# One attention and FFN layer, its instruction queues ordered by the framework's finer timeline model instead of its default model

## The chip, the cores and the metric

The kernel runs on one core of a Trainium2 chip. Five engines work from queues of their own, each in the order in which its instructions were written into it: TensorE (PE in the profile, with its weight loads as PEld), VectorE (DVE), ScalarE (ACT), GpSimd (POOL) and SyncE (SP), which issues the DMAs. An instruction that needs another engine's result waits on a semaphore, and everything behind it in its queue waits too. The metric is the device time of one execution in microseconds.

## The reference

One layer of a streaming encoder over 1024 positions of width 1024, all in float32. Two kinds of attention run on the same input, eight heads of 64 each:

```python
h = x @ w_in[l]
qa, ka, va, qb, kb, vb, ga, gb = jnp.split(h, split_pts, axis=-1)
y_a = chunk_band_attention(heads_a(qa), heads_a(ka), heads_a(va), rel_bias[l]) @ w_proj_a[l]
y_b = stick_breaking_attention(heads_b(qb), heads_b(kb), heads_b(vb)) @ w_proj_b[l]
gate_a = jax.nn.sigmoid(ga + b_gate[l, :D])
gate_b = jax.nn.sigmoid(gb + b_gate[l, D:])
mix = (gate_a * y_a + gate_b * y_b) @ w_out[l]
x = layer_norm(DEEPNORM_ALPHA * x + mix, ln1_g[l], ln1_b[l])
g, u = jnp.split(x @ w_ffn_in[l], 2, axis=-1)
x = layer_norm(DEEPNORM_ALPHA * x + (jax.nn.silu(g) * u) @ w_ffn_out[l], ln2_g[l], ln2_b[l])
```

Branch A is a softmax over a band of nine chunks of 64 keys with a learned bias by distance. Branch B is stick-breaking attention: the weight of a key is its sigmoid times the product of (1 - sigmoid) over the keys between it and the query, so it needs a running product along the keys.

## The kernel before, in words

Positions are stored backwards, so that a running product goes from left to right. For precision, each float32 operand of a product is split into a high part and a low remainder (`split`, L109 on ACT for the high part, L110 on DVE for the remainder), and a product is three matmuls: high by high, high by low, low by high. A matmul here has 128 x 128 weights and up to 512 columns.

The work goes in these stages, one after the other in the program's text:

1. *Input projection* (L171, tiles sxp, syp, szp). Blocks of columns of `w_in` are taken in pairs and multiplied by a scheme with seven products in place of eight (`pair_steps`). Pair 0 is multiplied plainly (L116 to L119, tile plain). The results q, k and v go to DRAM (q_dr, k_dr, v_dr), the first ten gate blocks too (g_dr).
2. *Attention*, sixteen heads: a0 to a7, then b0 to b7. Each head has eight *weight units* of 128 queries and twelve *value steps* of 128 keys.
   - A unit of branch A (`soft_block`): scores on TensorE (L464, L465, tile sc_a, PSUM banks of the tag sc, of which there are two), a DVE instruction that adds the bias and takes the row's minimum (L495), the exponential on ACT (L500), a reciprocal on DVE (L502), a scaling on POOL (L503).
   - A unit of branch B (`stick_block`): scores (tile sc_b), two sigmoids on ACT (L528, L529), the running products on DVE (L532, L536), a product on POOL (L538).
   - A value step: up to four transposes of weight blocks on TensorE (L561, tile tp), the split into pt (L109 on ACT, L110 on DVE), then two matmuls with v (L574, L575, tile pv). The two matmuls are written two steps behind their transposes (`LAG`). At a head's end ACT copies the sums out (L589), and a DMA and POOL join the halves into y (L590, L593, y_dr).
   - *Filler*: matmuls that belong to no head and are dealt out between the value steps by `fill_until`. There are 480: six gate blocks (L421, tile gps, 288 matmuls, each block with a weight load, a split by L404 and L405 and an eviction by L424), and the output product of branch A (L621, tile yAps, 192 matmuls), which needs the finished y of all eight heads of branch A, read back by `reload_y` (L644 to L648). `FILL = (18.0, 42.0)` gives 18 matmuls of filler to each head of branch A and 42 to each of branch B.
3. *Output product of branch B* and the gated sum (tile yBps, then L753, L754), *output projection* (tile ops), the first LayerNorm (POOL L769, ACT L777, POOL L778), and transposes of its result (L791, tile x1ps).
4. *Up projection* (tiles sxf, syf, szf), again with seven products for eight, 21 pairs and one plain block.
5. *Down projection* (L1049, tiles dx, dy, dz, with eighteen blocks by the seven-product scheme and four plain ones, tile fps), the second LayerNorm, and the output.

What sets the order: the program's text gives each instruction its place, and the framework's scheduler then orders each engine's queue. It lets the program run in a model that has a duration for each instruction, and at each point it takes, for an engine that is free, the earliest instruction of the text whose operands and tile slots are ready in the model. So the text's order is a priority and the model's durations decide who is ready. Tile slots are shared through tags (`SLOTS`, `BANKS`), and a later tile waits until the earlier one in its slot has been read for the last time.

## Time and profile before

| what | value |
|---|---|
| time of three runs | 1463.01, 1465.48, 1467.61 us, median 1465.48 |
| span of the profiled execution | 1464.5 us |
| TensorE busy | 1429.5 us (98%), 6740 matmuls |
| DVE busy | 1035.9 us (71%) |
| ACT busy | 679.2 us (46%) |
| POOL busy | 278.8 us (19%) |
| mean share of the 16 DMA engines | 50.6% for the one queue of the kernel's DMAs |
| mean granted TensorE clock | 0.997 |

The page gives no time for the profiled execution beside its span; the span is 1.0 us under the median of the runs. Matmuls are pipelined, so the duration of one overlaps its neighbours, and busy time of TensorE can be near 100% in a stretch where its matmuls start later than they could. The work of stretches is therefore better read from start times.

How the rows are read: in a group, "x96" is the number of instructions, then busy us and the mean ns of one, then idle time of the engine just before them and who ended it. In a row of a stretch, its length in us comes first, then busy us and the number of instructions of PE, PEld, DVE, ACT and POOL, then the granted clock, the DMA share and GB/s. In a row of the timeline or of the chain, the start and the length in us come first.

### The profile page before, as it was taken

How to read it: one execution, taken by the hardware profiler on the slowest of the kernel's cores; microseconds unless marked ns; L12 is line 12 of the kernel's file. 1: busy time of each engine (PE TensorE's matmuls, PEld its weight loads, DVE VectorE, ACT ScalarE, POOL GpSimd, SP SyncE). 2: the span in 40 equal slices, each digit the busy share in tenths (PEclk: the TensorE clock that was granted, in tenths of full speed). 3: DMA queues.
4: the chain of work that ended last, by engine and by line, in shares of the span. 5: the costliest groups of instructions: out<-in, count | busy, mean ns of one | idle time of the engine just before them, and what ended most of it. 6: DMA issues, size and time to landing. Idle time of an engine off the chain costs nothing.

```text
span 1464.5 us, 19170 instructions
## 1 busy us (share of the span) xinstructions
PE 1429.5 (98%) x6740; PEld 1181.3 (81%) x6740; DVE 1035.9 (71%) x1693; ACT 679.2 (46%) x1179; POOL 278.8 (19%) x326
## 2 busy tenths in 40 slices
PE   8999999999999998999999999999999999999997
PEld 6788888887888787777888888888888888888886
DVE  8856655434776987887848966777776665978767
ACT  6444444334887878775413534444444433221201
POOL 0000000003555779760004100000000000100016
PEclk9999999999999999999999999999999999999999
DMA  6555545328666476747611123444444456886602
GB/s 216 158 188 173 160 142 177 125 100 246 194 191 203 123 224 186 236 170 254 235 43 72 50 95 130 158 154 148 152 151 145 155 190 248 304 306 237 212 15 101
DMA packets 83455, 247.72 MB, mean 169 GB/s; under 512 B 10512, under 2 KB 10512, under 8 KB 83360
## 3 DMA queue, kind: packets, MB, share of 16 engines
q1 hardware_dynamic: 83360, 246.51, 50.6%
q8 instruction: 53, 0.87, 0.2%
q14 instruction: 42, 0.34, 0.1%
HBM read 162.03 MB, written 80.77 MB: 166 GB/s over the span
## 4 chain that ended last, share of the span: by engine, by line
PE 83%; DVE 7%; DMA 4%; ACT 2%; issue 2%; POOL 1%; SPq 0%; POOLq 0%; DVEq 0%; ACTq 0%
PE sxf L171 15%; PE sxp L171 12%; PE szf L171 8%; PE szp L171 6%; PE dx L1049 6%; PE syf L171 4%; PE gps L421 3%; PE dz L1049 3%; PE syp L171 3%; PE ops L119 2%; PE ops L117 2%; PE ops L116 2%; PE yAps L621 2%; PE dy L1049 1%; PE tp_b L561 1%
## 5 line engine op out<-in xcount | busy, mean ns | idle before, releaser
L1005 POOL TENSOR_TENSOR wdyt<-wdyt 128x512 f32<-128x512 f32 x8 | 10.9, 1366 | 513.6 <-DVE wdgt L1004 473.4
L538 POOL TENSOR_TENSOR w_b<-w_b,kp_b 128x511 f32<-128x511 f32 (+3 forms) x96 | 96.8, 1018 | 33.6 <-DVE kp_b L536 28.5
L536 DVE TENSOR_TENSOR_SCAN kp_b<-kp_b,ident_ps 128x384 f32<-128x384 f32 (+6 forms) x88 | 78.4, 891 | 7.0 <-ACT kp_b L528 2.2
L482 POOL MEMSET bias<- 64x64 f32 x8 | 1.2, 144 | 329.2 <-ACT bias L481 329.2
L184 DVE TENSOR_TENSOR c<-sxp,c 128x512 f32<-128x512 f32 x16 | 11.1, 692 | 74.6 <-issue 41.4
L769 POOL TENSOR_TENSOR mv<-mv,neghalf 128x1 f32<-128x1 f32 x16 | 23.8, 1489 | 209.4 <-DVE mv L768 209.4
L528 ACT ACTIVATE kp_b<-sc_b 128x512 f32<-128x512 f32 (+3 forms) x96 | 50.3, 525 | 24.0 <-PE sc_b L465 21.7
L110 DVE TENSOR_TENSOR pt_b<-tp_b,pt_b 128x512 fp32r<-128x512 f32 (+1 forms) x96 | 50.1, 541 | 12.5 <-ACT pt_b L109 12.3
L980 DVE TENSOR_TENSOR x<-dx,x 128x512 f32<-128x512 f32 x64 | 43.5, 687 | 17.0 <-PE dx L1049 16.9
L171 PE MATMUL szf<-x1S63h,wcf 128*128 128x512 f32 x168 | 55.1, 389 | 0.0
L109 ACT CAST pt_b<-tp_b 128x512 fp32r<-128x512 f32 (+1 forms) x96 | 48.4, 517 | 7.9 <-PE tp_b L561 7.3
L110 DVE TENSOR_TENSOR sl<-h,sl 128x512 fp32r<-128x512 f32 x56 | 38.4, 686 | 18.9 <-ACT sl L109 18.9
L503 POOL TENSOR_SCALAR w_a<-w_a,st_a 128x640 f32<-128x640 f32 (+2 forms) x64 | 42.6, 667 | 48.0 <-DVE st_a L502 29.7
L561 PE MATMUL tp_b<-ident,w_b 128*128 128x128 f32 x288 | 47.9, 275 | 3.4 <-DVE pt_b L110 3.1
L110 DVE TENSOR_TENSOR pt_a<-tp_a,pt_a 128x512 fp32r<-128x512 f32 (+1 forms) x96 | 46.0, 487 | 7.1 <-ACT pt_a L109 5.9
L529 ACT ACTIVATE w_b<-sc_b 128x511 f32<-128x511 f32 (+3 forms) x96 | 50.6, 527 | 0.0
L109 ACT CAST sl<-h 128x512 fp32r<-128x512 f32 x56 | 34.7, 619 | 33.5 <-PE syf L171 17.1
L116 PE MATMUL ops<-wh_o,mh 128*128 128x512 f32 x128 | 50.2, 392 | 0.0
L119 PE MATMUL ops<-wh_o,ml 128*128 128x512 f32 x128 | 50.0, 391 | 0.0
L117 PE MATMUL ops<-wl_o,mh 128*128 128x512 f32 x128 | 49.9, 390 | 0.0
L109 ACT CAST pt_a<-tp_a 128x512 fp32r<-128x512 f32 (+1 forms) x96 | 39.9, 425 | 19.2 <-PE tp_a L561 18.3
L500 ACT ACTIVATE w_a<-w_a,st_a 128x640 f32<-128x640 f32 (+2 forms) x64 | 44.7, 698 | 7.4 <-DVE st_a L495 5.7
(1883 smaller groups left out, 4796.5 us busy)
## 6 DMA issues: line engine op xcount, KB each, us to landing
s_dr<-sl SPq DMA_DIRECT2D x112, 256.0 KB, 2.2
sd<-s_dr SPq DMA_DIRECT2D x56, 512.0 KB, 4.8
wLf<-in_w_ffn_in_dram SPq DMA_DIRECT2D x22, 512.0 KB, 4.5
wRf<-in_w_ffn_in_dram SPq DMA_DIRECT2D x22, 512.0 KB, 3.5
wLp<-in_w_in_dram SPq DMA_DIRECT2D x17, 512.0 KB, 5.3
wRp<-in_w_in_dram SPq DMA_DIRECT2D x17, 512.0 KB, 4.2
v_dr<-v SPq DMA_DIRECT2D x16, 512.0 KB, 4.2
qs<-q_dr SPq DMA_DIRECT2D x16, 512.0 KB, 5.0
```

The lines of the kernel that those rows point to most:

```text
L109: nc.scalar.copy(dst_h, src)
L110: nc.vector.tensor_tensor(dst_l, src, dst_h.bitcast(F32), ALU.subtract)
L116: mm(acc, lh, rh, start=(i == 0), stop=False)
L117: mm(acc, lh, rl, start=False, stop=False)
L119: mm(acc, ll, rh, start=False, stop=(i == n))
L171: mm(acc, lw[:, ks], rx, start=(first and kt == i == 0), stop=(kt == 3 and i == 2), skip_group_check=not first)
L528: nc.scalar.activation(kp[:, c0:e], sc[:, 0:n], AF.Sigmoid, scale=-1.0)
L529: nc.scalar.activation(be[:, m0:e], sc[:, m0 - c0:n], AF.Sigmoid)
L536: nc.vector.tensor_tensor_scan(kp[:, s0:e], kp[:, s0:e], ident_ps()[:, 0:e - s0], kp[:, s0 - 1:s0], ALU.mult, ALU.bypass)
L538: nc.gpsimd.tensor_tensor(be[:, m0:e], be[:, m0:e], kp[:, m0 - 1:e - 1], ALU.mult)
L561: tr(tp[:, (qb - lo_q) * P:(qb - lo_q + 1) * P], wt[qb - q0][:, (kb - qb) * P:(kb - qb + 1) * P], ident)
L1049: mm(acc, a, b, start=(first and i == n == 0), stop=(i == n - 1 == 1), skip_group_check=not first)
```

## The change

One argument of the context that orders the program. The operations, their tiles, their engines and all sizes are the same; the scheduler's model of time is another, so the instructions of each engine's queue, and the semaphore waits that follow from that, stand in another order.

```diff
     o = nc.dram_tensor("out_0_dram", (1, S, D), F32, kind="ExternalOutput").ap()
-    with tile.TileContext(nc) as tc:
+    with tile.TileContext(nc, schedule_with_timeline_sim=True) as tc:
         hybrid_trunk_kernel(tc, **ap, out=o[0])
```

## The prediction

> **What bounds the kernel now.** I read the page first, for the engines' shares and the chain that ended last, then the busy time by stretch of time, then the groups of instructions by line inside the one stretch where TensorE is not full.
>
> ```profile
> span 1464.5 us, 19170 instructions
> PE 1429.5 (98%) x6740; PEld 1181.3 (81%) x6740; DVE 1035.9 (71%) x1693; ACT 679.2 (46%) x1179; POOL 278.8 (19%) x326
> ...
> PE 83%; DVE 7%; DMA 4%; ACT 2%; issue 2%; POOL 1%; SPq 0%; POOLq 0%; DVEq 0%; ACTq 0%
> ```
>
> ```profile
> 145.44 2.72 PE sxp L171 x12
> ```
>
> TensorE is busy 98% of the span and carries 83% of the chain. In the chain by time (second fence: start, length), twelve matmuls of 512 columns take 2.72 us: 0.227 us each is what a 512-column matmul costs when nothing is late. I call that its pitch. The 389 ns that the groups give for one overlaps its neighbours. Pitches of the narrower shapes come from a dense piece of the timeline, as differences of start times:
>
> ```profile
> 510.25 0.28 PE L574 MATMUL pv_b<-pt_b,v 128*128 128x256 f32 x1
> 510.37 0.28 PE L575 MATMUL pv_b<-pt_b,v 128*128 128x256 f32 x1
> ...
> 511.02 0.28 PE L465 MATMUL sc_b<-kl,qs 128*128 128x128 f32 x1
> 511.13 0.62 PE L561 MATMUL tp_b<-ident,w_b 128*128 128x128 f32 x4
> 511.51 0.47 PE L421 MATMUL gps<-xl,wh_g 128*128 128x512 f32 x1
> ```
>
> That is 0.12 us for 256 columns, about 0.09 for 128 and 0.095 for a transpose (four in 0.38); 320 and 384 columns lie between, 0.147 and 0.175. I add these up over any run of matmuls and call the sum the pure TensorE work of it. Now the stretches, one row each (length, then busy time of PE, PEld, DVE, ACT, POOL):
>
> ```profile
> 335.50:439.80 104.30, 100.61 (x591) 85.71 (x590) 73.32 (x266) 76.23 (x189) 53.23 (x73) 1.00 0.70 207
> 439.80:676.00 236.20, 222.91 (x1244) 185.45 (x1242) 188.56 (x362) 185.44 (x409) 163.19 (x208) 0.99 0.62 190
> 676.00:721.10 45.10, 44.89 (x196) 36.10 (x196) 38.30 (x54) 22.23 (x30) 0.00 (x0) 1.00 0.75 267
> 480.00:500.00 20.00, 17.20 (x100) 13.71 (x101) 18.83 (x34) 17.57 (x43) 16.49 (x26) 1.00 0.42 142
> ...
> 590.00:660.00 70.00, 64.59 (x362) 53.92 (x360) 60.03 (x102) 53.31 (x118) 48.10 (x64) 1.00 0.63 197
> 900.00:1200.00 300.00, 300.00 (x1325) 248.10 (x1324) 212.01 (x291) 129.17 (x195) 0.00 (x0) 1.00 0.44 157
> ```
>
> From 900 to 1200 (the up projection) TensorE is full for all 300 us: nothing can be won, only lost. The first three rows are the attention, cut at the 1450th, 2040th, 3280th and 3474th matmul in issue order; I call them stretch 1, 2 and 3. Their pure work is 91.6, 206.3 and 44.0 us, so they lose 12.7, 29.9 and 1.1 us. That is 43.7 us out of about 50 in the whole kernel; by the same sum the first 200 matmuls lose some 7.5, the stretch about the first LayerNorm about 2.5, all else nothing. What the change is worth is decided here.
>
> **What the change moves.** It removes and adds no computation, only the order in each queue differs: 5,396 of 6,740 matmuls stand at another place. Comparing the two instruction orders by kind:
>
> | matmuls | stretch 1 before | stretch 1 after | stretch 2 before | stretch 2 after |
> |---|---|---|---|---|
> | gps (gates, filler) | 96 | 288 | 192 | 0 |
> | yAps (filler) | 0 | 3 | 192 | 189 |
> | scores, branch A | 152 | 88 | 40 | 104 |
> | transposes tp_a | 164 | 90 | 76 | 150 |
> | values pv_a | 124 | 67 | 68 | 125 |
> | all of branch B | 0 | 0 | 672 | 654 |
>
> Before, the filler is dealt out evenly: the middle one of the 288 gps stands at place 2236, the last at 2725. After, they run in one rush from place 1482 to 2028, beside heads a0 to a2. Filler is work that can always run; it covers TensorE while an attention head waits for DVE, ACT and POOL. The other filler can't take its place at once: a yAps needs the y of all four branch A pairs, so places 2029 to 2538 (a3's rest, a4 to a7, half of b0) hold only 18 of them.
>
> *Stretch 1.* Pure work rises from 91.6 to 110.5 us. For each matmul that waits I counted, in both orders, how many matmuls lie between it and the last one that its producers had to wait for. Between places 1500 and 2000 the smallest such distance was 4 before and is 20 after (some 4 us of matmuls), so TensorE should run nearly full. Bounds: 110.5, and 110.5 plus the 12.7 lost there now; six gate weights have to arrive through SP, ACT and POOL in 110 us, against loads of half that. I take 112, nearest to the full rows: **+7.7**.
>
> *Stretch 2.* Pure TensorE work falls from 206.3 to 189.3, but the work of 2.5 branch A heads arrives (64/24 by scores, 74/30 by transposes, 57/24 by values). What eight of them cost the other engines:
>
> ```profile
> L110 DVE TENSOR_TENSOR pt_a<-tp_a,pt_a 128x512 fp32r<-128x512 f32 (+1 forms) x96 | 46.0, 487 | 7.1 <-ACT pt_a L109 5.9
> L495 DVE CUSTOM_DVE_ANT_0 w_a<-sc_a,bias 128x320 f32<-128x320 f32 (+2 forms) x64 | 30.8, 488 | 9.1 <-PE sc_a L465 7.3 <-PE tp_a L561 1.4
> L495 DVE CUSTOM_DVE_ANT_0 w_a<-sc_a,bias,st_a 128x320 f32<-128x320 f32 x32 | 17.6, 549 | 3.1 <-PE sc_a L465 1.8
> L502 DVE RECIPROCAL st_a<-st_a 128x1 f32<-128x1 f32 x64 | 10.4, 162 | 11.5 <-ACT w_a L500 10.8
> L495 DVE DVE_READ_ACCUMULATOR2_ANT st_a<- 128x1 f32 x96 | 8.0, 83 | 0.0
> ...
> L500 ACT ACTIVATE w_a<-w_a,st_a 128x640 f32<-128x640 f32 (+2 forms) x64 | 44.7, 698 | 7.4 <-DVE st_a L495 5.7 <-DVE st_a L502 0.5
> L109 ACT CAST pt_a<-tp_a 128x512 fp32r<-128x512 f32 (+1 forms) x96 | 39.9, 425 | 19.2 <-PE tp_a L561 18.3
> L500 ACT ACTIVATION_READ_ACCUMULATOR w_a<-w_a,st_a 128x1 f32 x64 | 12.1, 190 | 0.0
> L424 ACT COPY gate<-gps 128x512 f32<-128x512 f32 x12 | 7.5, 622 | 0.6 <-PE gps L421 0.6
> L404 ACT CAST wh_g<-wr_g 128x1024 fp32r<-128x1024 f32 x6 | 6.3, 1049 | 5.4 <-DMA wr_g<-in_w_in_dram 5.4
> L589 ACT COPY yv_a<-pv_a 128x512 f32<-128x512 f32 x8 | 4.7, 586 | 0.0
> L589 ACT COPY yt<-pv_a 128x512 f32<-128x512 f32 x8 | 4.6, 580 | 0.0
> ...
> L503 POOL TENSOR_SCALAR w_a<-w_a,st_a 128x640 f32<-128x640 f32 (+2 forms) x64 | 42.6, 667 | 48.0 <-DVE st_a L502 29.7 <-PE sc_a L465 9.4 <-PE tp_a L561 7.8
> L593 POOL TENSOR_TENSOR yt<-yt,yv_a 64x512 f32<-64x512 f32 x16 | 20.6, 1288 | 8.0 <-DMA yv_a<-yt 5.1 <-DMA yt<-yv_a 2.3
> L405 POOL TENSOR_TENSOR wl_g<-wr_g,wh_g 128x1024 fp32r<-128x1024 f32 x5 | 12.0, 2403 | 16.2 <-ACT wh_g L404 16.0 <-PE gps L421 0.2
> ```
>
> DVE: (46.0 + 30.8 + 17.6 + 10.4 + 8.0) / 8 = 14.1 us a head. ACT: 106 / 8 = 13.3. POOL: 63.2 / 8 = 7.9. In return the splits and evictions of four gates leave: ACT 4 × (1.05 + 2 × 0.62) = 9.2, POOL 4 × 2.4 = 9.6. So stretch 2 has to hold, beside 189 on TensorE:
> - DVE 188.6 + 2.5 × 14.1 = 223.9, less about 2 for the end of b7, which now stands behind the cut: 222;
> - ACT 185.4 + 33.2 − 9.2 = 209 (two more table loads, seven instead of five in all, add at most 2.6 and ACT isn't the longest);
> - POOL 163.2 + 19.8 − 9.6 = 173.
>
> The longest load passes from TensorE to DVE. Where TensorE sets the pace, DVE is busy 80% of stretch 2 and 86% of 590 to 660; where DVE sets it, at the start of branch B (480 to 500), 94%, for 20 us. And DVE has no filler: between places 2000 and 3250, 197 waiting matmuls now stand fewer than 12 matmuls behind what they need, against 45 before. I take 90%, the middle of 86 and 94: 222 / 0.90 = 246.7, **+10.5**. Ends: 94% gives 236 (0), 80% gives 278 (+41).
>
> *Stretch 3.* The last value products of b7 come behind the filler's end, and 18 yBps that could cover the drain now stand ahead of it: eviction (0.58), split of yh7 (1.12) and the add between are bare, about 3 us, on 42.2 of pure work: 45, **0**. Bounds −2 and +3.
>
> *Elsewhere.* In the projections, the up projection and the down projection matmuls are reordered within two neighbouring weight pairs, at most 13 us. The smallest distance rises there, from 4 to 7 or more in the input projection, from 12 to 22 in the up projection (12 are 2.7 us, several times the ACT copy or DVE add that they cover), from 18 to 23 in the down projection, so the cover stays: 0. One wait at the head of the up projection falls to 3, up to +1. In the first 60 us the halves of pair 0 are interleaved and three waits on freshly split weights are as bare as before; 0, bounds −4 and +4. Of the DMAs, the gates' loads and stores stand up to 154 us earlier on SP, ahead of the q, k and v loads of a1 to a5, whose slots come 15 to 35 us later, as the heads themselves do; the y reloads and gA loads now stand among the k loads of b0 to b4, and a late one holds up the head behind it. I put that into the 90%.
>
> Sum: 7.7 + 10.5 + 0 = +18.2 us on the profiled 1464.5. The runs' median, 1465.48, is 1.0 above that span; on it the forecast is 1484.
>
> **Rivals.**
> 1. *The order fits, and it gets faster.* The finer model knows the durations better, stretch 1 no longer loses 12.7 us, and in stretch 2 all four engines interleave without waits. Break-even is 385.6 − 112 − 45 = 228.6 us for stretch 2, a DVE share of 97%. Between 480 and 500 DVE 94%, ACT 88% and POOL 82% were busy together, which speaks for it; that it lasted 20 us speaks against. Faster needs less DVE work as well, by early work in stretch 1 that I can't see: at 215 to 224 us the kernel takes 1452 to 1461.
> 2. *No change.* A DVE share of 96 to 99%, 1461 to 1470. That the option does nothing is excluded by the table.
> 3. *TensorE's clock falls in the gaps.* The trace shows that once:
>
> ```profile
> 578.40 0.50 PE L574 MATMUL pv_b<-pt_b,v 128*128 128x512 f32 x1 [3.08 <-ACT yv_b L589]
> ...
> 580.00:582.00 2.00, 2.00 (x8) 1.71 (x7) 1.09 (x3) 2.00 (x5) 2.00 (x2) 0.50 0.06 14
> 582.00:584.00 2.00, 2.00 (x13) 1.82 (x12) 1.39 (x3) 1.61 (x4) 2.00 (x3) 0.84 0.00 0
> ```
>
> After a gap of 3.08 us the granted clock is 0.50 for about 3.4 us: 1.7 us of matmul time lost. TensorE will idle some 57 us in stretch 2 (246.7 − 189.3). In pieces under 3 us that costs nothing; if a third of it falls into six longer gaps, 6 × 1.7 = 10 us, and the kernel takes 1490 to 1515. Against it: only one gap of that length today.
> [...]
>
> **How the numbers follow.** About 0.3% (4.4 us) is what a measurement can tell from no change. The forecast, filler spent early and DVE setting the pace (5 to 41 us slower): 0.64. Rival 3: 0.08. Rival 1: 0.17. Rival 2: 0.11. So slower 0.72, same 0.11, faster 0.17. Range 1458 to 1511: it cuts off the faster end of rival 1 and the slowest of rival 3 and of the 80% end, about 1 in 10 on each side.
>
> **What would show it.** Right: gps rows end near 450 us, TensorE almost without gaps up to there; behind it PE busy near 77% and DVE near 90% until branch B ends; waits of PE on DVE and ACT (pt_a, pt_b, st_a) that hardly exist now. Wrong: stretch 2 under 229 us, or TensorE gaps in the up or down projection, where I put nothing, or a late gate weight in stretch 1.

## The result, and the profile after

The changed kernel takes 1518.18 us (median of 5 runs, 1514.50 to 1524.22) against 1465.68 us of the kernel before in the same comparison: 1.035 times as long, 95% interval 1.0334 to 1.0365. The forecast was 1484 us with a range to 1511. The direction was right, and the size was about a third of the real one: on the profiled spans the change costs 1515.4 - 1464.5 = 50.9 us, and the prediction's sum was 18.2.

First the page of the changed kernel (span, shares of the engines, shares of the chain), then its busy time by stretch, cut at the same matmuls as in the prediction (length, then busy time of PE, PEld, DVE, ACT, POOL, then granted clock, DMA share, GB/s):

```profile
span 1515.4 us, 19144 instructions
PE 1450.7 (96%) x6740; PEld 1191.7 (79%) x6740; DVE 1020.6 (67%) x1693; ACT 679.0 (45%) x1181; POOL 276.3 (18%) x326
...
PE 85%; DVE 6%; DMA 4%; ACT 3%; issue 1%; SPq 1%; POOL 0%; POOLq 0%; DVEq 0%; ACTq 0%
```

```profile
338.10:454.20 116.10, 114.07 (x592) 96.04 (x592) 43.28 (x148) 57.72 (x122) 40.29 (x45) 1.00 0.56 176
454.20:717.50 263.30, 226.28 (x1240) 180.75 (x1239) 210.44 (x473) 202.77 (x474) 174.07 (x235) 0.97 0.59 178
717.50:769.70 52.20, 47.32 (x198) 37.02 (x197) 38.56 (x57) 22.59 (x31) 0.00 (x0) 0.93 0.69 242
```

The page hardly tells the two kernels apart. The stretches do: ahead of the attention 338.1 - 335.5 = +2.6, stretch 1 +11.8, stretch 2 +27.1, stretch 3 +7.1, behind it +2.3; the sum is the 50.9. In stretch 2 DVE is busy 210.4 / 263.3 = 80%, the share that it had before (188.6 / 236.2), so DVE does not set the pace there. The granted clock is below 1.00 now in stretches 2 and 3 (0.97 and 0.93).

What TensorE waits for, in the changed kernel (total us, times, longest):

```profile
PE tp_b L561 <- DVE pt_b L110: 14.0, 27, 1.2
...
PE yAps L621 <- ACT yh L647: 4.7, 2, 3.2
PE tp_a L561 <- DVE pt_a L110: 3.7, 8, 1.4
...
PE yBps L116 <- ACT yh L109: 2.5, 1, 2.5
```

The first of these rows in the kernel before:

```profile
PE tp_b L561 <- DVE pt_b L110: 3.1, 5, 0.9
```

And what ACT waits for from DMAs in the attention, in the changed kernel and then in the kernel before:

```profile
ACT wh_g L404 <- DMA wr_g<-in_w_in_dram: 17.1, 5, 5.0
...
ACT yh L647 <- DMA yraw<-y_dr: 9.2, 3, 4.2
...
ACT gA L653 <- DMA gA<-g_dr: 6.9, 4, 2.5
```

```profile
ACT wh_g L404 <- DMA wr_g<-in_w_in_dram: 5.4, 2, 3.4
...
ACT gA L653 <- DMA gA<-g_dr: 4.0, 2, 2.6
ACT yh L647 <- DMA yraw<-y_dr: 3.7, 1, 3.7
```

In these three rows 33.2 us against 13.1: the instructions that read a freshly loaded tile (gate weights, reloaded y, reloaded gates) reach the head of ACT's queue before their load has landed, and wait there. That is the line the prediction had not looked for. One such place of the changed kernel, on ACT and then on TensorE (start, length, in brackets the idle time before and what ended it):

```profile
493.62 0.56 ACT L109 CAST pt_a<-tp_a 128x512 fp32r<-128x512 f32 x1
497.97 1.04 ACT L647 CAST yh<-yraw 128x1024 fp32r<-128x1024 f32 x1 [3.79 <-DMA yraw<-y_dr]
498.92 0.75 ACT L109 CAST pt_a<-tp_a 128x384 fp32r<-128x384 f32 x2
```

```profile
495.62 0.27 PE L561 MATMUL tp_a<-ident,w_a 128*128 128x128 f32 x1
499.07 0.96 PE L621 MATMUL yAps<-yh,wh_y 128*128 128x512 f32 x2 [3.17 <-ACT yh L647]
```

ACT stands still for 3.79 us while the casts of a5 wait behind the cast of y. TensorE stops for 3.17 us on filler, on work that was to cover waits: the yAps of place 2262 was started before its y was there.

### The profile page after: what moved, and what is told of

It reads as the page before. It is cut to its first block, busy times and chain, and to the rows that moved or that the text cites. A ratio compares the mean times of both kernels' runs of the same rounds, so it can differ in the third digit from the quotient of the medians.

```text
span 1515.4 us, 19144 instructions
## 1 busy us (share of the span) xinstructions
PE 1450.7 (96%) x6740; PEld 1191.7 (79%) x6740; DVE 1020.6 (67%) x1693; ACT 679.0 (45%) x1181; POOL 276.3 (18%) x326
## 4 chain that ended last, share of the span: by engine, by line
PE 85%; DVE 6%; DMA 4%; ACT 3%; issue 1%; SPq 1%; POOL 0%; POOLq 0%; DVEq 0%; ACTq 0%
PE sxf L171 15%; PE sxp L171 11%; PE szf L171 8%; PE szp L171 6%; PE dx L1049 6%; PE gps L421 4%; PE syf L171 4%; PE dz L1049 3%; PE syp L171 3%; PE yAps L621 2%; DVE kp_b L536 2%; PE ops L119 2%; PE ops L116 2%; PE ops L117 2%; PE fpswh_h L119 1%
## 5 line engine op out<-in xcount | busy, mean ns | idle before, releaser
L561 PE MATMUL tp_b<-ident,w_b 128*128 128x128 f32 x288 | 51.5, 291 | 16.3 <-DVE pt_b L110 14.0
L482 POOL MEMSET bias<- 64x64 f32 x8 | 1.2, 144 | 335.7 <-ACT bias L481 335.7
L561 PEld LDWEIGHTS tp_b<-ident,w_b 128*128 128x128 f32 x288 | 34.8, 146 | 32.7 <-DVE pt_b L110 20.0
L109 ACT CAST pt_b<-tp_b 128x512 fp32r<-128x512 f32 (+1 forms) x96 | 46.5, 501 | 18.3 <-PE tp_b L561 17.9
L188 ACT COPY gt<-sxf 128x512 f32<-128x512 f32 x21 | 12.3, 592 | 87.0 <-PE sxf L171 87.0
L561 PE MATMUL tp_a<-ident,w_a 128*128 128x128 f32 x240 | 44.9, 279 | 4.7 <-DVE pt_a L110 3.7
```

Source lines behind the costliest of these rows:

```text
L109: nc.scalar.copy(dst_h, src)
L561: tr(tp[:, (qb - lo_q) * P:(qb - lo_q + 1) * P], wt[qb - q0][:, (kb - qb) * P:(kb - qb + 1) * P], ident)
```

## The experiments

Theory P, the prediction's: the loss is filler used up early in TensorE's queue, with DVE setting the pace behind it. A rival, S: the loss comes from TensorE's order at the seams (start, yB, LayerNorm). A third one came up during the work. Theory D: the finer model sets *readers of loads* too far ahead in ACT's queue (and POOL's), and they hold up the attention's casts and exponentials.

All runs in one table. Columns: median, ratio to the kernel before of the same comparison with its 95% interval, then from one profiled execution the start of the 1450th matmul and the length of the stretches up to the 2040th, 2400th, 3280th and 3474th (start times of these matmuls in the trace), and what follows them. Times in us.

| kernel | median | ratio | to 1450 | to 2040 | to 2400 | to 3280 | to 3474 | rest |
|---|---|---|---|---|---|---|---|---|
| before | 1465.68 | | 335.5 | 104.3 | 66.3 | 169.9 | 45.1 | 743.4 |
| changed | 1518.18 | 1.035 (1.0334 to 1.0365) | 338.1 | 116.1 | 71.8 | 191.5 | 52.2 | 745.7 |
| default_rush | 1480.33 | 1.0083 (1.0066 to 1.0099) | 336.1 | 114.5 | 66.3 | 173.1 | 45.0 | 743.5 |
| pin_fill | 1496.65 | 1.0192 (1.0175 to 1.021) | 338.3 | 113.2 | 73.9 | 168.9 | 51.6 | 746.3 |
| seams | 1518.57 | 1.0339 (1.0321 to 1.0356) | 338.4 | 115.5 | 73.0 | 192.4 | 46.5 | 751.8 |
| pin_seams | 1499.67 | 1.022 (1.0198 to 1.0242) | 337.8 | 113.2 | 74.4 | 174.1 | 46.4 | 751.4 |
| pe_before | 1507.19 | 1.0262 (1.0235 to 1.0289) | 342.8 | 111.9 | 72.2 | 181.7 | 47.4 | 751.6 |
| pe_after | 1538.56 | 1.0487 (1.046 to 1.0514) | 340.7 | 116.7 | 75.7 | 206.5 | 50.9 | 746.2 |
| fill_after | 1526.46 | 1.0398 (1.0376 to 1.042) | 335.3 | 118.0 | 81.2 | 201.1 | 46.6 | 743.3 |
| fill_before | 1506.62 | 1.0259 (1.0236 to 1.0283) | 337.5 | 115.4 | 70.8 | 184.5 | 52.0 | 744.1 |
| pe_keep | 1482.01 | 1.0102 (1.0087 to 1.0117) | 340.9 | 103.4 | 66.7 | 163.6 | 46.4 | 760.4 |
| pe_act | 1488.70 | 1.0147 (1.0131 to 1.0162) | 341.6 | 105.5 | 66.4 | 169.1 | 46.2 | 758.4 |
| pe_rest | 1482.44 | 1.0111 (1.0092 to 1.0131) | 336.2 | 106.3 | 69.9 | 171.8 | 48.3 | 746.1 |
| pe_sp | 1504.82 | 1.0255 (1.0239 to 1.027) | 348.3 | 108.5 | 70.8 | 175.0 | 47.7 | 752.3 |
| after_keep | 1505.49 | 1.0252 (1.0232 to 1.0272) | 338.9 | 109.8 | 68.0 | 180.9 | 53.0 | 750.6 |
| three | 1483.75 | 1.0102 (1.0079 to 1.0125) | 338.0 | 110.8 | 65.8 | 170.3 | 47.5 | 752.0 |
| held_mix | 1462.16 | 0.9954 (0.9939 to 0.9968) | 336.0 | 102.1 | 66.7 | 164.7 | 45.2 | 743.3 |
| before_later | 1466.51 | 0.9987 (0.9978 to 0.9997) | 335.7 | 105.3 | 66.3 | 169.4 | 45.4 | 743.3 |

**The prediction's mechanism alone.** The default model, with the gates' matmuls dealt out by hand so that they run in the same rush (places 1508 to 2039, and the 19th yAps at 2552, where the changed kernel has 2538):

```diff
-FILL = (18.0, 42.0)
+FILL = (115.0, 115.0, 57.5) + (0.0,) * 6 + (25.5,) * 6 + (41.0,)
...
-        goal += FILL[hd["br"]] / nhead
+        goal += FILL[hidx] / nhead
```

> The kernel before with its default model, but FILL is changed so that the text itself spends the gates' filler early (115, 115 and 57.5 matmuls in a0, a1 and a2, none in a3 to b0, then 25.5 a head and 41 in b7); places of gps 1508 to 2039 and of the 18th yAps 2552 are nearly those of the changed kernel (1482 to 2028, 2538). Theory 1: stretch 1 110 to 117 us, stretch 2 252 to 270, the kernel 1497 to 1515, with the start and the up projection as before. Rival 2: the default model's order has longer distances, so stretch 2 stays under 245 and the kernel under 1485.

The rush costs 12 us at the median: stretch 1 +10.2, matmuls 2040 to 3280 +3.2, where the prediction had 7.7 and 10.5. The expected 1497 to 1515 us was missed; time and stretch 2 (239.4 us) came out as named for the rival, the default model's longer distances. (The part without filler loses 9.3 between 2400 and 2700, and between 2700 and 3000, where more filler is left, 6.0 come back.) So the mechanism exists. With the default model's order it makes a quarter of the loss, two thirds of the prediction's 18.2 in sum and divided otherwise between the stretches; how much it makes in the finer model's order this run does not show.

**The filler held back in the changed kernel.** Each filler matmul is ordered behind the attention matmul that precedes it in the text:

```diff
             try:
-                state["t"] += next(fill)
+                with tc.issue_after(tens["last"].ins):
+                    state["t"] += next(fill)
```

(`tens["last"]` is the last matmul or transpose written so far.)

> The changed kernel, but each filler matmul (gps, yAps) is kept in TensorE's queue behind the attention matmul that precedes it in the text; all else is ordered by the finer model. Theory 1 (the finer model spends the gates' filler in a rush beside heads a0 to a2, and stretch 2 then has nothing to cover TensorE): stretch 1 falls from 116 us to 103 to 107, stretch 2 from 263 to 232 to 242, stretch 3 from 52 to about 47; the 3 us at the start and the 3.6 us at the head of the up projection stay, so 1470 to 1478. Rival 2 (the finer model's close handovers between the engines cost the time, wherever the filler stands): stretch 2 stays over 255, and the kernel over 1505.

Matmuls 2400 to 3280 are back at the time of before (168.9 against 169.9). Up to 2400 nothing is won: 187.1 us for 1450 to 2400 against 170.6 before. The attention takes 407.6 us, 24.0 less than in the changed kernel. In branch B the loss was filler placement, in branch A something else. Neither expectation was met: 1496.65 us lies between 1478 and 1505.

**The seams.** In the changed kernel, pair 0's evictions are ordered behind pair 1's splits on DVE, the yBps behind the last value product of b7, and the plain block of the up projection behind the transposes of x1; then the same with the filler held back as well.

```diff
-            mm3(acc, [(w[0][:, ks], w[1][:, ks], yh[4 + k][:, cs], yl[4 + k][:, cs])
...
+            with tc.issue_after(last_value.ins):
+                mm3(acc, [(w[0][:, ks], w[1][:, ks], yh[4 + k][:, cs], yl[4 + k][:, cs])
```

> The changed kernel with its filler left in the rush, but three other places are put back into the text's order: the evictions of pair 0 on DVE stand behind the splits of pair 1, the yBps stand behind b7's last value product, and plainhl_0f stands behind the last transposes of the first LayerNorm's result. Theory 1: these are separate small losses; the start falls by 2 to 3 us, stretch 3 by 3 to 5, the head of the up projection by 3, so 1507 to 1511, and stretch 2 stays at 258 to 266. If instead the seams are only where a delay from elsewhere comes to light, the kernel stays within 3 us of 1518.

> Both edits together: filler kept at its place in the text, and the three seams put back. Theory 1: the two add up, everything the finer model lost is back, 1462 to 1470 (the kernel before: 1465.7). Rival 2: over 1495.

The yB seam gives back what it had lost (52.2 to 46.5). The start does not move. The third edit gives back the 3.6 us of matmuls 4000 to 4100 (22.7 us again) and loses 9.7 just ahead of them, between 3800 and 4000, so behind the attention 6 us more are lost than in the changed kernel, and neither total gets better (1518.57 against 1518.18, 1499.67 against 1496.65). Both expectations for theory 1 (1507 to 1511, and 1462 to 1470 us) were missed. Of rival S some 6 us are left, at one place.

**One queue at a time.** The next kernels chain the instructions of a queue in a recorded order by dependencies that order the issue and add no wait (shortened here; in the kernels the orders are packed). Text and model stay; the scheduler arranges the queues that are not held around the held one.

```diff
+QUEUES = {"PE": ...}      # instruction numbers in the order of the other kernel's queue
+def hold_queues(tc):
+    traced = {i.name: i for i in tc.nc.cur_bb.bb.instructions}
+    for numbers in QUEUES.values():
+        prev = None
+        for n in numbers:
+            ins = traced[f"I-{n}"]
+            if prev is not None:
+                tc.add_manual_dep(ins, prev.name, ...)
+            prev = ins
...
         hybrid_trunk_kernel(tc, **ap, out=o[0])
+        hold_queues(tc)
```

First TensorE's queue, in four ways: the finer model with the order of before (`pe_before`), the default model with the changed order (`pe_after`), and with the filler's places from one kernel and the other matmuls' order from the other.

> The changed kernel, with TensorE's queue held in the order of the kernel before, matmul for matmul; the other four queues stay with the finer model, which orders them around the held one. Theory Q (the loss is made in TensorE's queue): 1466 to 1473 us, the waits of tp_b on pt_b as rare as before, half clock under 7 us. Theory O (the loss that was left with the filler pinned, some 29 us, comes from the other queues: late k loads on SP, late splits on DVE and ACT): 1485 to 1497 us, with the gaps at sc_a0 and sc_a1 still there. Half of each would be near 1480.

> The mirror of that: the kernel before, with TensorE's queue held in the order of the changed kernel; the other four queues are ordered by the default model. Theory Q: 1512 to 1525 us. Theory O: 1483 to 1495 us, the filler's part of the loss alone. Together with the run that holds the order of before it tells whether the two parts add up: the two runs' losses should sum to some 52 us where they do.

> The kernel before, with the 480 filler matmuls at the places in TensorE's queue that they have in the changed kernel, and all others in the order of before; the other queues are ordered by the default model. If the places of both fillers carry the loss of branch B (21.7 us between matmuls 2400 and 3280) and the rush adds its 10 us in front: 1492 to 1500 us, stretches 2400 to 3280 together at 185 to 192 us instead of 170. If the order of the attention's own matmuls is needed too: no more than the 1480 of the rush of gates alone, 2400 to 3280 at 170 to 177.

> The changed kernel, with the 480 filler matmuls at the places in TensorE's queue that they have in the kernel before, and all others in the changed kernel's order; the other queues stay with the finer model. It repeats the run with the filler pinned in another way: 1490 to 1500 us if the order of the attention's own matmuls (or the other queues) carries the rest, with 2400 to 3280 near 169 us; 1470 to 1476 us if the filler's places carry nearly all and the pinned run lost by what it pinned them to.

This broke the frame of both theories. With TensorE's queue exactly that of before, the finer model's other four queues still cost 39 us, more than theory O's 29. With the filler at the changed places and all else by the default model the loss is 58 us, with TensorE's whole changed order 70. The losses do not add to 52, and all four mixtures of the two orders are worse than expected. That each model's queues fit each other, and a queue of the one does not fit those of the other, would explain it and was not tested by itself. The filler's places alone are enough for a loss in branch B (201.1 us against 169.9 for 2400 to 3280).

In `pe_before` only 409 of ACT's 1110 instructions stand at another place than before, and most of them moved by no more than 5 places. The readers of loads moved furthest: a cast wh_g stands 39 places further ahead, three sigmoids of gA 21 to 26 (places counted by kind of instruction in the two traces). The commonest exchanges: the sigmoids of gA stand ahead of casts and sigmoids of branch B in 80 pairs, the casts wh_g ahead of casts and exponentials of branch A in 51. What the sigmoid of gA3 does, 25 places further ahead, on ACT and on TensorE:

```profile
605.95 0.27 ACT L529 ACTIVATE w_b<-sc_b 128x127 f32<-128x127 f32 x1
610.70 1.15 ACT L653 ACTIVATE gA<-gA,bg 128x1024 f32<-128x1024 f32 x1 [4.47 <-DMA gA<-g_dr]
611.75 0.57 ACT L109 CAST pt_b<-tp_b 128x512 fp32r<-128x512 f32 x1
612.22 0.59 ACT L589 COPY yv_b<-pv_b 128x512 f32<-128x512 f32 x1
```

```profile
612.86 0.51 PE L574 MATMUL pv_b<-pt_b,v 128*128 128x512 f32 x1 [3.98 <-ACT yv_b L589]
```

ACT waits 4.47 us for a load; a cast and a copy of branch B stand behind; the copy (of b3) is what frees the PSUM bank of the next value product, and TensorE stops for 3.98 us. The gate loaded here, gA3, is first used by DVE at 649.7 us, 39 us later. That is theory D, and it can be tested without a change to TensorE's queue.

**Readers of loads.** `pe_keep` is `pe_before` with one more constraint: an instruction of ACT, DVE or POOL that reads a loaded tile goes behind the nearest non-readers (up to three) that it follows in the kernel before. `pe_act`, `pe_rest` and `pe_sp` hold whole queues beside TensorE's: ACT's; all but ACT's (on DVE without the instructions of L495, which its trace shows at other places than before); SP's.

```diff
+BEHIND = (...)            # pairs: reader of a loaded tile, instruction ahead of it in before's queue
...
+    for reader, ahead in BEHIND:
+        tc.add_manual_dep(traced[f"I-{reader}"], f"I-{ahead}", ...)
```

> The changed kernel with TensorE's queue held in the order of before (that alone took 1507 us), and beside it one more constraint on ACT, DVE and POOL: an instruction that reads a tile which a DMA has loaded (casts of gate and projection weights, the casts of reloaded y, the sigmoids of reloaded gates, the joining adds of y) does not stand further ahead in its queue than in the kernel before. Everything else in these queues stays with the finer model. Theory D (the finer model takes loads for landed sooner than they land, sets their readers ahead of the attention's own work, and they hold up an in-order queue): the attention (matmuls 1450 to 3474), 30 us over before in the run without this, loses at most 8 of them, and the kernel takes 1478 to 1487 us. Theory E (the loss comes from the order of splits, exponentials and scans among themselves): 1500 to 1510.

> The changed kernel with TensorE's and ACT's queues both held in the order of before; DVE, POOL and SP stay with the finer model. If ACT's order carries what the run with TensorE alone lost (39 us): 1470 to 1480 us. If it is DVE, POOL or SP: 1495 to 1510.

> The complement: all queues but ACT's held in the order of before, ACT's alone ordered by the finer model. If ACT's order carries the loss: 1495 to 1507 us, with ACT's waits for DMA (wh_g, gA, yh) near the 28 us of the run with TensorE held alone, against 13 before. If it does not: 1466 to 1475.

> The changed kernel with TensorE's and SP's queues held in the order of before. If the loads themselves are issued too late (k loads behind the gates' loads): 1475 to 1490 us. If the loads are issued in time and their readers stand too early (theory D), or if it is the order of the attention's work: 1500 to 1510.

Theory D was the one borne out, and its number with it: 1482.01 us, and the attention (1450 to 3474) takes 380.1 us where it took 413.2 without the constraint and 385.6 before. Of ACT's waits for gate weights, y and gA, 27.7 us in the first three rows below (`pe_before`), the last row (`pe_keep`) is the largest that is left:

```profile
ACT wh_g L404 <- DMA wr_g<-in_w_in_dram: 14.7, 5, 3.3
...
ACT yh L647 <- DMA yraw<-y_dr: 6.7, 2, 5.4
...
ACT gA L653 <- DMA gA<-g_dr: 6.3, 4, 4.5
```

```profile
ACT wh_g L404 <- DMA wr_g<-in_w_in_dram: 5.4, 2, 3.5
```

The readers are not all that moved between the two (63 of SP's 650 places differ too), but ACT's whole order does nearly the same for the attention (387.2, with 57 of SP's places different; its total, 1488.70, missed the expected 1470 to 1480). So with TensorE's order held, the loss in the attention goes with ACT's order.

The other two runs limit this. `pe_rest` loses 10.7 us in the attention (396.3) and takes 1482.44 us, not the expected 1495 to 1507, and its three waits of ACT come to 11.0 us, not to some 28. But the scheduler also arranged ACT anew around the held queues: the cast wh_g that stands 39 places ahead in `pe_before` stands 10 ahead here. `pe_sp`, with SP's order of before, takes 11 of the 27.6 us off the attention (402.0), though the total hardly moves, because the start gets longer; in it the same cast also stands only 10 places ahead. So how far a load's time of issue has a part of its own is open. Outside the attention these mixtures lose up to 22 us (`pe_keep`: 5.4 at the start, 17.0 behind), with ACT's or the readers' order held most of it in the up projection, which says nothing about the change.

**The changed kernel with its own TensorE order.** `after_keep` is the changed kernel with the readers held back and nothing else. `three` adds the filler (not ahead of the attention matmul that it follows in the kernel before) and the yBps (behind the last value product of b7).

```diff
+BEHIND = (...)            # after_keep: readers; three: readers, filler and yBps
...
         hybrid_trunk_kernel(tc, **ap, out=o[0])
+        hold_queues(tc)
```

> The changed kernel, TensorE's queue free again, with one constraint alone: a reader of a loaded tile on ACT, DVE and POOL does not stand ahead of the non-readers that it follows in the kernel before. TensorE's order then follows from the finer model: the gates' matmuls stand at places 1470 to 2411 (middle one 1805), the yAps at 2702 to 3273, nearly where they were before the change. Theory D alone (both the early fillers and the stalled ACT queue come from readers that the finer model sets too early): the attention is back within 6 us of before, and what stays is the start (+3) and the head of the up projection (+3): 1470 to 1482 us. Theory P (the order of the attention's own matmuls costs the 17 us of branch A that the pinned filler did not give back): 1486 to 1500.

> The changed kernel with three one-sided constraints and nothing else held: each filler matmul does not stand ahead of the attention matmul that it follows in the kernel before; readers of loaded tiles on ACT, DVE and POOL as in the run with them alone (1505 us); the yBps not ahead of the last value product of b7. The attention's own matmuls, splits, exponentials and scans stay in the finer model's order. If filler places, readers and the seam are the whole loss of the attention: stretches 1450 to 3474 at 380 to 392 us (before 385.6, changed 431.6), and with the start (+3) and the head of the up projection (+3) 1466 to 1478 us. If the finer order of the attention's own work costs something by itself, as the filler-pinned run's 17 us of branch A seemed to say: 1484 to 1496.

With the readers held, the attention goes from 431.6 to 411.7 us, and 2040 to 2400 is within 1.7 us of before. Not all of this is ACT's waits: with the readers TensorE's filler moved as well, and the gates' matmuls, which ended at place 2028, now end at 2411. What is left is what theory P describes: they end at place 2411 and the yAps start at 2702, and in that hole 2400 to 2700 takes 69.3 us, against 53.2 before. The expected 1470 to 1482 us was missed by that hole (16 us), the yB seam (7.9) and 5 us more behind the attention than in the changed kernel.

With all three put back the attention takes 394.4 us: 37.2 of the 46.0 us that it had lost are accounted for, and matmuls 2040 to 3280 take 236.1 us, before 236.2. The finer order of the attention's own work costs nothing there. Still over: 6.5 us up to matmul 2040 (TensorE waits 4.0 for a k load there, the row below) and 2.4 at the yB seam, 2.5 at the start and 8.6 behind the attention, where in the changed kernel it was 2.3. The expected 1466 to 1478 us was missed by these; they were not followed further.

```profile
PE sc_a L465 <- DMA kl<-k_dr: 4.0, 1, 4.0
```

**A version that is faster than both, and the kernel before looked at again.** `held_mix` is `pe_keep` with all five queues in the order of before outside the attention. `before_later` is the kernel before with five readers moved back on ACT.

```diff
+LATER = ((2833, 2713), (3470, 2713), (6112, 5888), (6290, 6199), (6945, 6755))
+    for reader, ahead in LATER:      # wh_g11, wh_g12, yh4, gA3, gA7
+        tc.add_manual_dep(traced[f"I-{reader}"], f"I-{ahead}", ...)
```

> The run with TensorE's order and the readers held (1482 us), with all five queues held in the order of before outside the attention; inside it ACT, DVE, POOL and SP stay with the finer model. There that run was 5.5 us faster than before (380.1 us against 385.6) and it lost 19 us at the start and in the up projection by the other queues' order. If the stretches add up: 1458 to 1464 us, faster than both kernels. If the input projection's order set up the attention's gain, or the gain was chance: 1466 to 1472.

> The kernel before, default model, with five readers of loads moved further behind on ACT: wh_g11 and wh_g12, yh4, gA3 and gA7, which waited for their DMA for 3.4, 0, 3.7, 2.6 and 1.4 us at the head of the queue; 59 matmuls change their place. Theory D holds for the kernel before too: the one gap of TensorE with half clock (3.08 us at 578) goes, 3 to 8 us in all: 1458 to 1464 us. If ACT's waits there were covered by TensorE's other work: 1465 to 1469.

`held_mix` takes 1462.16 us against 1468.18 in the same comparison, ratio 0.9954 (0.9939 to 0.9968): faster than both kernels, by the 7 us that its attention is shorter. Its attention as one stretch (columns as above), 378.7 us where before takes 385.6, at a granted clock of 1.00 as before:

```profile
336.00:714.70 378.70, 368.01 (x2026) 307.62 (x2025) 299.81 (x680) 282.80 (x627) 215.82 (x280) 1.00 0.69 207
```

`before_later` gains 0.13%, less than a measurement can tell, and not the expected 1458 to 1464 us. The timeline of ACT gives a reason. In the kernel before, yh4 holds ACT for 3.73 us:

```profile
576.44 1.04 ACT L647 CAST yh<-yraw 128x1024 fp32r<-128x1024 f32 x1 [3.73 <-DMA yraw<-y_dr]
```

In `before_later`, with yh4 behind the next head's work, wh_y is the next reader in the queue and waits 5.42 us at the same place. The wait was passed on, not removed:

```profile
581.05 1.04 ACT L404 CAST wh_y<-wr_y 128x1024 fp32r<-128x1024 f32 x1 [5.42 <-DMA wr_y<-in_w_proj_dram]
```

In `held_mix` SP issued the load of yraw4 at 563.7 and ACT read it at 571.1; before, these were 569.8 and 576.4. That the earlier issue is the reason for its gain was not tested.

## Why the prediction was right in its direction and wrong in its size

*Stretch 1, +7.7 predicted, +11.8 measured.* The pure work of 110.5 us was right, and TensorE runs nearly full (5.6 us lost, 1.5 taken). The rush by the default model gives 114.5, nearly the same.

*Stretch 2, +10.5 predicted, +27.1 measured: the step that failed.* "I take 90%, the middle of 86 and 94" rested on DVE setting the pace. Its load was smaller than worked out (210.4 us, not 222), and at 90% of the stretch it would have made no loss at all. It was busy 80%, the share of the prediction's slow end (+41 with its larger load), and TensorE lost some 74 us there (263.3 - 189.3), not 57. What set the pace were waits in queues that are worked off in order: with filler, readers of loads and yBps put back (`three`), matmuls 2040 to 3280 take 236.1 us again. The waits of tp_b on pt_b came as foreseen (3.1 to 14.0 us), and the hole without filler is real: 16 us in `after_keep`, undone in branch B by `pin_fill`.

*What the step left out.* "a late one holds up the head behind it. I put that into the 90%": the loads were looked at on SP and not at their readers on ACT. The prediction counted in TensorE's queue how far a waiting matmul stands behind what it needs, and it did no such count for ACT, where a reader of a load moved up to 39 places ahead (`pe_before`) and the longest waits of ACT for a load were 3 to 5 us. Put back in the changed kernel, the readers give 19.9 us of the attention's 46.0, the move of the filler that comes with it included; between `pin_seams` and `three`, which hold filler and seam in somewhat different ways, they give 13.7. The filler held back alone gives 24.0 (`pin_fill`). The parts overlap, and how the 46.0 divide among them stays open.

*Stretch 3, 0 predicted (-2 to +3), +7.1 measured.* The 18 yBps were seen to stand ahead of the drain, and the conclusion that about 3 us stay bare was wrong: the first yBps waits 2.5 us for yh7, with two shorter gaps before it, and the clock falls (0.50 from 724.7 to 731.5 us, 0.93 over the stretch). With the yBps put behind the last value product the stretch takes 46.5.

*Elsewhere, 0 predicted, +2.6 and +2.3 measured.* Inside the bounds of 4 us for the start. At the head of the up projection the single wait that was to cost up to 1 us costs 3.6 (26.3 us against 22.7 for matmuls 4000 to 4100). Up and down projection: 0, as predicted.

*Rival 3* had a chance of 0.08 and took part. The clock is at half for 23.9 us in the attention, 3.4 before, which by halves is up to 12 us of matmul time. It was put down as an alternative to the forecast, but each of its five falls there stands behind a gap of TensorE (1.58 to 3.44 us from start to start), and it comes on top. "In pieces under 3 us that costs nothing" agreed with the kernel before, where a gap of 2.81 us from start to start, at 602 us, left the clock at 1.00; for the changed kernel it was wrong, as the last section shows.

*Rival 2* has a slip in its sum: by 222 us of DVE, shares of 96 to 99% give 1461 to 1468 us, not 1470. Nothing else rests on it.

## What to carry to other kernels

When a scheduler's model changes, compare every engine's queue, not the bottleneck's alone, and look first for the instructions that read a load: if one of them moves forward in an in-order queue (here by up to 39 places), what is left of its load time can land on everything behind it (here in waits of up to 5.4 us), however unhurried the reader itself is. Filler has to last as long as the work that it covers (the hole without it cost 16 us in `after_keep`), and a filler matmul that itself waits stops the queue that it was to fill (3.17 us at one yAps of the changed kernel). Orders can be tested one queue at a time with dependencies that only order the issue, but the scheduler rearranges the queues that are not held, and most mixtures here missed what was expected of them, so the sum of such runs is not the sum of the causes.

## What the runs showed of the hardware

In the changed kernel the clock fell behind a gap much shorter than the 3.08 us that the prediction had seen. Rows of TensorE and then the granted clock (last but two of a row) around 700 us:

```profile
698.49 0.38 PE L574 MATMUL pv_b<-pt_b,v 128*128 128x256 f32 x1
700.07 0.63 PE L561 MATMUL tp_b<-ident,w_b 128*128 128x128 f32 x4 [1.20 <-DVE pt_b L110]
```

```profile
698.00:700.00 2.00, 0.65 (x3) 0.45 (x3) 1.97 (x5) 1.50 (x7) 1.34 (x2) 1.00 0.88 300
700.00:702.00 2.00, 1.93 (x12) 1.64 (x12) 1.83 (x5) 1.21 (x2) 1.78 (x3) 0.70 1.04 306
702.00:704.00 2.00, 1.12 (x5) 0.77 (x5) 1.32 (x4) 1.95 (x5) 1.86 (x2) 0.50 0.96 336
704.00:706.00 2.00, 2.00 (x8) 1.81 (x7) 1.67 (x4) 2.00 (x4) 0.76 (x1) 0.50 0.78 299
```

From start to start less the pitch of 256 columns (0.12 us) the gap is 1.46 us; the clock falls at 700.8 us and stays at 0.50 for 6.8 us. A longer single gap, in `pe_before`, left the clock at 1.00 (start to start 2.62 us, less 0.23 for 512 columns: 2.39):

```profile
578.17 0.39 PE L465 MATMUL sc_b<-kl,qs 128*128 128x512 f32 x1
580.79 0.50 PE L464 MATMUL sc_b<-kh,qs 128*128 128x512 f32 x1 [2.23 <-ACT w_b L529]
```

```profile
580.00:582.00 2.00, 1.21 (x7) 1.06 (x8) 1.11 (x2) 2.00 (x7) 2.00 (x1) 1.00 1.06 289
582.00:584.00 2.00, 2.00 (x12) 1.66 (x11) 1.43 (x2) 2.00 (x5) 2.00 (x3) 1.00 0.97 329
```

So in these two traces the length of the single gap does not tell whether the clock falls: it fell behind 1.46 us and stayed at 1.00 behind 2.39. In the profile of the changed kernel, the last 6 us of its span left out, the clock is at 0.50 seven times, four times for 3.4 us and three times for 6.8; in the kernel before, with the same end left out, once, for 3.4 us. What sets the gaps with a fall apart from those without was not shown.
